# Value products of a chunked attention: from pairs of token tiles to all four at once

## The chip, the cores and the metric

The kernel runs on one core of one Trainium2 chip. The metric is the device time of one execution in microseconds (us). Lower is better. The kernel before was timed three times; its median is 1318.02 us.

A core has engines that run beside each other and meet only at semaphores: TensorE (PE, matrix products; its weight loads are listed as PEld), VectorE (DVE), ScalarE (ACT), GpSimd (POOL) and SyncE (SP, which here issues nearly all transfers). Each takes its instructions in the order in which they are written for it. PE writes its products into PSUM, eight banks of 512 fp32 columns; all else lies in SBUF or in DRAM.

## The reference

One layer of a hybrid encoder over 2048 tokens of width 1024. A normalised input goes through one wide projection, whose columns feed three mixers: chunked softmax attention (6 heads of 64), an mLSTM (6 heads) and gated linear attention (4 heads). Each is gated, the results are put side by side, projected back, added to the input and normalised. The change touches the attention:

```python
# q, k, v: 6 heads of 64; a chunk is 64 tokens; a query sees its own chunk and 8 chunks before it
scores = einsum('bnqhd,bnkhd->bhnqk', qc, kb) * d ** -0.5
scores = where(valid, scores + rel_bias, -1e30)
p = softmax(scores)                       # over up to 9 * 64 keys
o = einsum('bhnqk,bnkhd->bnqhd', p, vb)   # "value products" below
y_a = o * silu(gate)
out = rmsnorm(x + concat(y_a, y_b, y_c) @ w_out)
```

## The kernel before

**Stages.** The 2048 tokens are four quarters (`q` = 0 to 3, `QT` = 512 tokens), each of four token tiles (`tt` = 0 to 3) of 128. In the first stage, which ends at about 913 us of the profiled span, each quarter is projected and the two recurrent mixers run; queries, keys, values and gates are written to DRAM. The second stage is the attention and the output projection. Every fp32 factor is there as two parts, high and low (`FR`, fp32r), and a product is the sum of two or three products of parts.

**Order on PE.** PE's order is the order in which the program emits its instructions (`manual_schedule`, line 134). Generators yield after each piece and `merge(a, b, na, nb)` (line 76) interleaves two of them: a counter starts at 0, goes up by `nb` for a step of `a` and down by `na` for a step of `b`; `a` steps while it is not positive. The order on the other engines is set by a planner that simulates a timeline.

**The attention of one head** has two generators:

- `scores(q, h)` (line 936) loads the head's queries, keys and values, and per token tile makes the products with its keys (line 960): for `q` of 1 to 3 each tile has 640 keys, in two segments of 384 and 256 columns, with a bank of the pool `s` (two banks) each. VectorE adds the bias and takes the maximum (976), ScalarE the exponential and its sum (979), VectorE the reciprocal (980), GpSimd scales the tile `pt` (981). 8 steps for a head.
- `mix(q, h)` (line 1001) takes the four `pt` tiles, transposes their 128x128 blocks on PE into a bank `tp` (1032, three banks), copies it as high part `ph` (1037, ScalarE) and low part `pl` (1038, VectorE), three buffers each, and multiplies them with the values `vv` into the bank `w` (one bank): line 1046 with `ph` and 128 columns of weights, line 1049 with `pl` and 64. When the head is done, its two halves are added into `cc` (1052 on ScalarE, 1053 on VectorE), and after every second head `cc` is gated (1067) and split into the two parts of `Y` (997, 998). A filled `tp` is called a pack; the value products of a pack come two packs after its transposes.

For `q` of 1 to 3 the four token tiles cover eight key blocks of 128: tile `tt` needs the blocks `tt` to `tt + 4`, 20 blocks for a head. Before the change `mix` works on pairs of tiles (0 and 1, then 2 and 3). A block that both tiles of a pair need is one product of 256 columns, any other one of 128. Six packs for a head, of 512, 512 and 256 columns for each pair; 24 value products.

**Groups of heads.** `attention0` does quarter 0 (mixed with the last projections) and the scores of the first head of quarter 1. Then, for `q` = 1, 2, 3, `attention(q)` merges `scores(q, h)` with `mix(q, h - 1)`, and `spread` merges the whole with `out_mm(q - 1)`, the output projection of the quarter before: 64 steps of three products with 512 columns (1099 to 1101), "o" below. `spread` is told how many attention steps there will be (`units * 14 + 8 * (units - 1)`); what it doesn't use up of `out_mm` comes at the end of the quarter, with no attention beside it. `load_y` (1119) then fetches the other mixers' results for the next `out_mm` through two buffers `wraw`, splits them into `Y[3]` to `Y[7]` (997 on ScalarE, 998 on GpSimd), and these take the place of the quarter's before, which the last steps of `out_mm` still read.

Of the kernel before, what the change touches and what calls it, by code (L numbers as in the profile page):

```python
# [11 lines left out]
ALU = mybir.AluOpType  # L12
# [60 lines left out]

def merge(a, b, na, nb):
    acc = 0
    live = True
    while a is not None or b is not None:
        if a is not None and (b is None or acc <= 0):  # L80
            acc += nb
            try:
                next(a)
                yield
            except StopIteration:
                a = None
        elif b is not None:
            acc -= na
            try:
                next(b)  # L90
                yield
            except StopIteration:
                b = None
# [6 lines left out]
def f32(ap):  # L100
    return ap.bitcast(FP32)
# [3 lines left out]
def trunk_kernel(ctx: ExitStack, tc: tile.TileContext, xT, x, w_f, w_t, w_o, w_gates, norm_g, conv_w,  # L105
# [760 lines left out]
    with ExitStack() as pb_:  # L866
# [134 lines left out]
        def mix(q, h, Y, vv, pts, nkb):  # L1001
# [4 lines left out]
                cur["gt"] = big.tile([P, QT], FP32, name="gt")  # L1006
                nc.sync.dma_start(cur["gt"], ga_d[:, h // 2, q * QT:(q + 1) * QT])
            cc, gt = cur["cc"], cur["gt"]
            todo = []
            for pr in range(NC // 2):  # L1010
                pp = pts[2 * pr:2 * pr + 2]
                one_use, two_use = [], []
                for b in range(nkb):
                    use = tuple(tt for tt in range(2) if pp[tt][1] <= b < pp[tt][1] + pp[tt][2])
                    if use:
                        (one_use if len(use) == 1 else two_use).append((b, use))
                packs, width = [], 1024
                for b, use in one_use + two_use:
                    if width + P * len(use) > 512:
                        packs.append([])  # L1020
                        width = 0
                    packs[-1].append((b, use, width))
                    width += P * len(use)
                todo += [(pr, pp, g, pk, g == len(packs) - 1) for g, pk in enumerate(packs)]
            ops = {}

            def turn_(pr, pp, g, pk, last):
                tp = pbank("tp")
                for b, use, w in pk:
                    for x_, tt in enumerate(use):  # L1030
                        pt, b0, _ = pp[tt]
                        nc.tensor.transpose(out=tp[:, w + x_ * P:w + (x_ + 1) * P],  # L1032
                                            in_=pt[:, (b - b0) * P:(b - b0 + 1) * P], identity=ident)
                wd = pk[-1][2] + P * len(pk[-1][1])
                ph = big.tile([P, 512], FR, name="ph", bufs=3)
                pl = big.tile([P, 512], FR, name="pl", bufs=3)
                nc.scalar.copy(ph[:, :wd], tp[:, :wd])  # L1037
                nc.vector.tensor_tensor(pl[:, :wd], tp[:, :wd], f32(ph[:, :wd]), op=ALU.subtract)  # L1038
                return ph, pl

            def pv(pr, pp, g, pk, last, ph, pl):
                if not ops:
                    ops[0] = pbank("w")
                op = ops[0][:, pr * ST:(pr + 1) * ST]
                for e, (b, use, w) in enumerate(pk):
                    nc.tensor.matmul(op[:, use[0] * P:use[0] * P + P * len(use)], vv[:, b, :], ph[:, w:w + P * len(use)],  # L1046
                                     start=(pr == 0 and g == 0 and e == 0), stop=False, skip_group_check=True)
                for e, (b, use, w) in enumerate(pk):
                    nc.tensor.matmul(op[0:64, use[0] * P:use[0] * P + P * len(use)], vv[:, b, 64 * (h % 2):64 * (h % 2) + 64],  # L1049
                                     pl[:, w:w + P * len(use)], start=False, stop=(last and e == len(pk) - 1), skip_group_check=True)  # L1050
                if last and pr == NC // 2 - 1:
                    nc.scalar.copy(cc[mr], ops[0][cr])
                    nc.vector.tensor_tensor(cc[mr], ops[0][mr], cc[mr], op=ALU.add)

            held = []
            for it in todo:
                ph, pl = turn_(*it)
                yield
                held.append(it + (ph, pl))
                if len(held) > 2:  # L1060
                    pv(*held.pop(0))
                    yield
            pv(*held.pop(0))
            yield
            pv(*held.pop(0))
            if h % 2 == 1:
                nc.gpsimd.tensor_tensor(cc, cc, gt, op=ALU.mult)
                Y[h // 2] = split_y(cc, q, h // 2)
# [13 lines left out]
        def attention(q, Y, done):  # L1082
            for h in range(len(done), AH + 1):
                a = scores(q, h, done) if h < AH else None
                b = mix(q, h - 1, Y, *done[h - 1]) if h else None
                yield from merge(a, b, 8, 14)

        def out_mm(q, Y):
            for tt in range(NC):
# [46 lines left out]
        for q in range(1, NQ):  # L1136
            YB = {}
            units = AH + 1 - len(nxt)
            spread(attention(q, YB, nxt), units * 14 + 8 * (units - 1), out_mm(q - 1, YA), YN)
            nxt = []  # L1140
            YA = YB
            for k in (3, 4, 5, 6, 7):
                load_y(q, YA, k)
# [85 lines left out]
```

## Time and profile before

| | |
|---|---|
| median of 3 runs | 1318.02 us (1317.06 to 1320.14) |
| the profiled execution's own time | 1321.42 us |
| its span, from which the profile counts | 1319.7 us |
| PE busy | 1266.8 us (96%) |
| DVE, POOL, ACT busy | 813.0, 630.6, 595.9 us |
| mean granted clock of PE | 0.982 |

Reading it: PE's times are starts and lengths of instructions that overlap each other, as a product's tail runs under the next one's head; what a product costs a full PE is the distance from its start to the start of the next. A wait is shown as `[us <-who released it]`. The number after `x` is how many like instructions were put into one row. PEclk is the granted clock of PE as a share of the full one.

### The profile page before, as it was taken

The numbers are of one execution on the slowest core, as the hardware profiler recorded it, in microseconds if no ns is written. First come the engines' busy times: TensorE is split into PE (matmuls) and PEld (weight loads), VectorE is DVE, ScalarE is ACT, GpSimd is POOL, SyncE is SP. The second block draws the span as 40 slices with busy tenths as digits, with TensorE's granted clock in tenths as the row PEclk, the third lists the DMA queues.
The fourth block names the chain that finished last, engine by engine and source line by source line (L and its number), as shares of the span: only waits on it lengthen the run. The fifth ranks groups of instructions, "written<-read, shape, count | busy, mean of one in ns | idle before, by whom it ended". The sixth has DMA issues, their size and how long they took to land.

```text
span 1319.7 us, 19935 instructions
## 1 busy us (share of the span) xinstructions
PE 1266.8 (96%) x7044; PEld 1038.1 (79%) x7044; DVE 813.0 (62%) x1859; ACT 595.9 (45%) x1124; POOL 630.6 (48%) x847
## 2 busy tenths in 40 slices
PE   4999999999999999999999999999979999999997
PEld 2788777878787788877778787887768888889876
DVE  7626656672775767267666866664467767666711
ACT  5624422463443247244224543332466556556621
POOL 5327652332766225367622656642165454454442
PEclk7999999999999999999999999999889999999999
DMA  7444233634423354442244333328677656565222
GB/s 249 157 120 136 84 104 113 181 121 138 129 80 106 111 183 133 127 134 86 91 127 125 112 102 88 108 69 260 180 221 218 184 176 187 157 206 148 81 95 79
DMA packets 106516, 181.66 MB, mean 138 GB/s; under 512 B 9776, under 2 KB 54704, under 8 KB 106416
## 3 DMA queue, kind: packets, MB, share of 16 engines
q1 hardware_dynamic: 101808, 172.00, 43.6%
q10 hardware_dynamic: 4608, 8.39, 1.7%
q8 instruction: 55, 0.90, 0.3%
q14 instruction: 45, 0.37, 0.1%
HBM read 143.92 MB, written 36.44 MB: 137 GB/s over the span
## 4 chain that ended last, share of the span: by engine, by line
PE 81%; DVE 8%; DMA 3%; ACT 3%; issue 2%; POOL 2%; SPq 1%; POOLq 0%; DVEq 0%; ACTq 0%
PE ip L245 13%; PE ip L247 12%; PE ip L246 12%; PE ip L1101 4%; PE ip L1099 4%; PE ip L1100 4%; PE ip L265 3%; PE s L960 3%; PE ip L267 3%; PE ip L266 3%; PE tp L1032 3%; PE w L1049 2%; PE w L1046 2%; PE ga L748 2%; PE s L600 1%
## 5 line engine op out<-in xcount | busy, mean ns | idle before, releaser
L245 PE MATMUL ip<-x,w 128*128 128x512 f32 x800 | 329.2, 412 | 0.0
L247 PE MATMUL ip<-x,w 128*128 128x512 f32 x800 | 314.4, 393 | 0.0
L246 PE MATMUL ip<-x,w 128*128 128x512 f32 x800 | 313.6, 392 | 0.0
L245 PEld LDWEIGHTS ip<-x,w 128*128 128x128 f32 x800 | 151.3, 189 | 42.0 <-issue 12.9
L247 PEld LDWEIGHTS ip<-x,w 128*128 128x128 f32 x800 | 150.9, 189 | 33.4
L246 PEld LDWEIGHTS ip<-x,w 128*128 128x128 f32 x800 | 151.5, 189 | 29.0 <-issue 2.2
L238 DVE TENSOR_TENSOR w<-wraw,w 128x1024 fp32r<-128x1024 f32 x88 | 122.8, 1395 | 70.0 <-ACT w L237 64.2
L237 ACT CAST w<-wraw 128x1024 fp32r<-128x1024 f32 x132 | 137.9, 1046 | 60.4 <-DMA wraw<-in_w_f 27.6
L238 POOL TENSOR_TENSOR w<-wraw,w 128x1024 fp32r<-128x1024 f32 x44 | 107.8, 2449 | 79.3 <-ACT w L237 79.3
L981 POOL TENSOR_SCALAR pt<-pt,sm 128x640 f32<-128x640 f32 (+2 forms) x96 | 71.2, 743 | 135.8 <-DVE sm L980 110.5
L265 PE MATMUL ip<-w,x 128*128 128x512 f32 x256 | 101.9, 398 | 4.9 <-ACT vg L429 4.7
L267 PE MATMUL ip<-w,x 128*128 128x512 f32 x256 | 99.9, 390 | 0.0
L266 PE MATMUL ip<-w,x 128*128 128x512 f32 x256 | 99.8, 390 | 0.0
L979 ACT ACTIVATE pt<-pt,sm 128x640 f32<-128x640 f32 (+2 forms) x96 | 73.3, 763 | 52.9 <-DVE sm L976 51.8
L691 POOL TENSOR_TENSOR prd<-gk,zg 128x16 f32<-128x16 f32 (+7 forms) x112 | 66.1, 590 | 60.6 <-PE pw L697 55.2
L960 PE MATMUL s<-kk,qq 128*128 128x256 f32 (+2 forms) x360 | 83.9, 320 | 5.7 <-DMA kk<-k_d 2.4
L1038 DVE TENSOR_TENSOR pl<-tp,ph 128x512 fp32r<-128x512 f32 (+2 forms) x126 | 73.9, 597 | 22.8 <-ACT ph L1037 21.5
L1037 ACT CAST ph<-tp 128x512 fp32r<-128x512 f32 (+2 forms) x126 | 63.1, 512 | 41.8 <-PE tp L1032 37.9
L400 ACT ACTIVATE e<-ip 128x512 f32<-128x512 f32 x44 | 26.1, 593 | 122.6 <-PE ip L247 106.3
L960 PEld LDWEIGHTS s<-kk,qq 128*128 128x128 f32 x360 | 63.5, 198 | 16.1 <-issue 5.2
L688 POOL TENSOR_TENSOR gk<-gk,al 128x16 f32<-128x16 f32 (+14 forms) x120 | 71.2, 594 | 8.5 <-ACT al L665 1.3
L470 DVE SCALAR_TENSOR_TENSOR qk<-u,cw,qk 128x512 f32<-128x512 f32 x72 | 69.7, 969 | 8.9 <-ACT qk L468 7.5
(303 smaller groups left out, 2544.8 us busy)
## 6 DMA issues: line engine op xcount, KB each, us to landing
wraw<-in_w_f SPq DMA_DIRECT2D x100, 512.0 KB, 3.6
wraw<-in_w_t SPq DMA_DIRECT2D x32, 512.0 KB, 3.7
qq<-q_d SPq DMA_DIRECT2D x48, 256.0 KB, 5.8
kk<-k_d SPq DMA_DIRECT2D x18, 512.0 KB, 6.8
vv<-v_d SPq DMA_DIRECT2D x18, 512.0 KB, 4.9
xraw<-in_x SPq DMA_DIRECT2D x16, 512.0 KB, 5.9
xraw<-in_xT SPq DMA_DIRECT2D x16, 512.0 KB, 6.8
xr<-in_x SPq DMA_DIRECT2D x16, 512.0 KB, 3.6
```

The lines of the kernel that those rows point to most:

```text
L237: nc.scalar.copy(w[:, :, 0, :], rv)
L238: other().tensor_tensor(w[:, :, 1, :], rv, f32(w[:, :, 0, :]), op=ALU.subtract)
L245: nc.tensor.matmul(ps, w[:, k, 0, :], X[k][:, 0, :], start=(k == 0), stop=False)
L246: nc.tensor.matmul(ps, w[:, k, 0, :], X[k][:, 1, :], start=False, stop=False)
L247: nc.tensor.matmul(ps, w[:, k, 1, :], X[k][:, 0, :], start=False, stop=(k == KT - 1))
L265: nc.tensor.matmul(ps, X[k][:, 0, t], w[:, 0, :], start=(k == 0), stop=False)
L266: nc.tensor.matmul(ps, X[k][:, 0, t], w[:, 1, :], start=False, stop=False)
L267: nc.tensor.matmul(ps, X[k][:, 1, t], w[:, 0, :], start=False, stop=(k == KT - 1))
L688: nc.gpsimd.tensor_tensor(b16(gk)[:, :, 0:c], b16(gk)[:, :, 0:c], b16(al)[:, :, c:c + 1].broadcast_to([P, NB, c]), op=ALU.mult)
L960: nc.tensor.matmul(sp[:, :cn], qq[:, l, tt * P:(tt + 1) * P], kk[:, ko + c0:ko + c0 + cn], start=(l == 0), stop=(l == 1))
L979: nc.scalar.activation(pt[:, :n], pt[:, :n], AF.Exp, bias=init, scale=-1.0, accum_out=sm[:, 2:3])
L1038: nc.vector.tensor_tensor(pl[:, :wd], tp[:, :wd], f32(ph[:, :wd]), op=ALU.subtract)
```

## The change

`mix` no longer works on pairs of tiles. For each of the eight key blocks it lists the tiles that need it (`use`), and a block is one product over all of them: 128, 256, 384, 512, 512, 384, 256, 128 columns for the blocks 0 to 7. The blocks are put into five packs of 512 columns each, in the order [2, 0], [1, 6], [3], [4], [5, 7]; in quarter 0, where there are four blocks of 512, 384, 256 and 128 columns, into [0], [1, 3], [2]. So a head has 16 value products instead of 24 (8 instead of 12 in quarter 0), five casts and subtractions of a pack instead of six (three and three), and as many transposes as before. The first pack needs the tiles 0 to 2, the second all four.

`mix` has 10 steps instead of 12 for `q` of 1 to 3, so `merge` in `attention` is given 10 instead of 14, and a counter that starts at -12: two steps of the scores come ahead of the first step of `mix`. `spread` is told of `units * 10` instead of `units * 14` steps. The bank `w` is taken at the start of `mix`. And the space that is reserved at the bottom of each SBUF partition for descriptors of dynamic DMA, 16,384 bytes by default, is set to 4,096, so what lies above it starts 12,288 bytes lower.

```diff
@@ -73,8 +73,7 @@
 
 
 
-def merge(a, b, na, nb):
-    acc = 0
+def merge(a, b, na, nb, acc=0):
     live = True
     while a is not None or b is not None:
         if a is not None and (b is None or acc <= 0):
@@ -1006,63 +1005,52 @@
                 cur["gt"] = big.tile([P, QT], FP32, name="gt")
                 nc.sync.dma_start(cur["gt"], ga_d[:, h // 2, q * QT:(q + 1) * QT])
             cc, gt = cur["cc"], cur["gt"]
-            todo = []
-            for pr in range(NC // 2):
-                pp = pts[2 * pr:2 * pr + 2]
-                one_use, two_use = [], []
-                for b in range(nkb):
-                    use = tuple(tt for tt in range(2) if pp[tt][1] <= b < pp[tt][1] + pp[tt][2])
-                    if use:
-                        (one_use if len(use) == 1 else two_use).append((b, use))
-                packs, width = [], 1024
-                for b, use in one_use + two_use:
-                    if width + P * len(use) > 512:
-                        packs.append([])
-                        width = 0
-                    packs[-1].append((b, use, width))
-                    width += P * len(use)
-                todo += [(pr, pp, g, pk, g == len(packs) - 1) for g, pk in enumerate(packs)]
-            ops = {}
-
-            def turn_(pr, pp, g, pk, last):
+            use = [[tt for tt in range(NC) if pts[tt][1] <= b < pts[tt][1] + pts[tt][2]] for b in range(nkb)]
+            packs = ([2, 0], [1, 6], [3], [4], [5, 7]) if q else ([0], [1, 3], [2])
+            src, done = {}, []
+            op = pbank("w")
+
+            def turn_(pk):
                 tp = pbank("tp")
-                for b, use, w in pk:
-                    for x_, tt in enumerate(use):
-                        pt, b0, _ = pp[tt]
+                w = 0
+                for b in pk:
+                    for x_, tt in enumerate(use[b]):
+                        pt, b0, _ = pts[tt]
                         nc.tensor.transpose(out=tp[:, w + x_ * P:w + (x_ + 1) * P],
                                             in_=pt[:, (b - b0) * P:(b - b0 + 1) * P], identity=ident)
-                wd = pk[-1][2] + P * len(pk[-1][1])
+                    src[b] = slice(w, w + P * len(use[b]))
+                    w += P * len(use[b])
                 ph = big.tile([P, 512], FR, name="ph", bufs=3)
                 pl = big.tile([P, 512], FR, name="pl", bufs=3)
-                nc.scalar.copy(ph[:, :wd], tp[:, :wd])
-                nc.vector.tensor_tensor(pl[:, :wd], tp[:, :wd], f32(ph[:, :wd]), op=ALU.subtract)
-                return ph, pl
-
-            def pv(pr, pp, g, pk, last, ph, pl):
-                if not ops:
-                    ops[0] = pbank("w")
-                op = ops[0][:, pr * ST:(pr + 1) * ST]
-                for e, (b, use, w) in enumerate(pk):
-                    nc.tensor.matmul(op[:, use[0] * P:use[0] * P + P * len(use)], vv[:, b, :], ph[:, w:w + P * len(use)],
-                                     start=(pr == 0 and g == 0 and e == 0), stop=False, skip_group_check=True)
-                for e, (b, use, w) in enumerate(pk):
-                    nc.tensor.matmul(op[0:64, use[0] * P:use[0] * P + P * len(use)], vv[:, b, 64 * (h % 2):64 * (h % 2) + 64],
-                                     pl[:, w:w + P * len(use)], start=False, stop=(last and e == len(pk) - 1), skip_group_check=True)
-                if last and pr == NC // 2 - 1:
-                    nc.scalar.copy(cc[mr], ops[0][cr])
-                    nc.vector.tensor_tensor(cc[mr], ops[0][mr], cc[mr], op=ALU.add)
+                nc.scalar.copy(ph[:, :w], tp[:, :w])
+                nc.vector.tensor_tensor(pl[:, :w], tp[:, :w], f32(ph[:, :w]), op=ALU.subtract)
+                for b in pk:
+                    src[b] = ph[:, src[b]], pl[:, src[b]]
+
+            def to(b, r=slice(0, P)):
+                return op[r, use[b][0] * P:use[b][0] * P + P * len(use[b])]
+
+            def pv(pk):
+                for b in pk:
+                    nc.tensor.matmul(to(b), vv[:, b, :], src[b][0], start=not done, stop=False, skip_group_check=True)
+                    done.append(b)
+                for b in pk:
+                    nc.tensor.matmul(to(b, slice(0, 64)), vv[:, b, 64 * (h % 2):64 * (h % 2) + 64], src[b][1],
+                                     start=False, stop=(len(done) == nkb and b == pk[-1]), skip_group_check=True)
 
             held = []
-            for it in todo:
-                ph, pl = turn_(*it)
+            for pk in packs:
+                turn_(pk)
                 yield
-                held.append(it + (ph, pl))
+                held.append(pk)
                 if len(held) > 2:
-                    pv(*held.pop(0))
+                    pv(held.pop(0))
                     yield
-            pv(*held.pop(0))
+            pv(held.pop(0))
             yield
-            pv(*held.pop(0))
+            pv(held.pop(0))
+            nc.scalar.copy(cc[mr], op[cr])
+            nc.vector.tensor_tensor(cc[mr], op[mr], cc[mr], op=ALU.add)
             if h % 2 == 1:
                 nc.gpsimd.tensor_tensor(cc, cc, gt, op=ALU.mult)
                 Y[h // 2] = split_y(cc, q, h // 2)
@@ -1083,7 +1071,7 @@
             for h in range(len(done), AH + 1):
                 a = scores(q, h, done) if h < AH else None
                 b = mix(q, h - 1, Y, *done[h - 1]) if h else None
-                yield from merge(a, b, 8, 14)
+                yield from merge(a, b, 8, 10, -12)
 
         def out_mm(q, Y):
             for tt in range(NC):
@@ -1136,7 +1124,7 @@
         for q in range(1, NQ):
             YB = {}
             units = AH + 1 - len(nxt)
-            spread(attention(q, YB, nxt), units * 14 + 8 * (units - 1), out_mm(q - 1, YA), YN)
+            spread(attention(q, YB, nxt), units * 10 + 8 * (units - 1), out_mm(q - 1, YA), YN)
             nxt = []
             YA = YB
             for k in (3, 4, 5, 6, 7):
@@ -1222,7 +1210,7 @@
 
     arrays = _layout(inputs)
     S = arrays["x"].shape[0]
-    nc = _bacc.Bacc("TRN2", target_bir_lowering=False, num_devices=1)
+    nc = _bacc.Bacc("TRN2", target_bir_lowering=False, num_devices=1, dynamic_dma_scratch_size=4096)
     _build(nc, arrays, S)
     r = _run(nc, [{f"in_{n}": v for n, v in arrays.items()}], core_ids=[0])
     return r.results[0]["out_0"].reshape(1, S, D)
```

## The prediction

> **What bounds the kernel now.** I read the page's head and chain, then the busy times by stage, PE's waits, and PE's instructions in order of time.
>
> ```profile
> span 1319.7 us, 19935 instructions
> PE 81%; DVE 8%; DMA 3%; ACT 3%; issue 2%; POOL 2%; SPq 1%; POOLq 0%; DVEq 0%; ACTq 0%
> ```
>
> ```profile
> 913.00:995.00 82.00, 70.13 (x367) 59.92 (x367) 46.18 (x150) 44.11 (x101) 31.66 (x38) 0.85 0.77 229
> ...
> 1078.00:1169.00 91.00, 88.49 (x552) 77.77 (x551) 61.47 (x183) 54.33 (x119) 45.21 (x47) 1.00 0.62 176
> ...
> 1262.00:1312.00 50.00, 47.21 (x195) 37.02 (x193) 8.99 (x21) 10.45 (x23) 17.41 (x17) 0.97 0.25 85
> ```
>
> After each stretch and its length come the busy times of PE, PEld, DVE, ACT and POOL, PEclk, DMA share and GB/s. PE is the chain. Where the attention runs beside the output projection (the middle row, quarter 2) PE is busy for 88.5 of 91 us, DVE for 61.5, ACT for 54.3, POOL for 45.2. So only two things can move the time: PE's own work, and its waits.
>
> ```profile
> PE w L1049 <- DVE pl L1038: 5.5, 6, 2.7
> PE w L1046 <- DVE cc L1053: 2.8, 1, 2.8
> PE s L960 <- DMA kk<-k_d: 2.4, 1, 2.4
> ...
> PE ip L1099 <- ACT y L997: 2.0, 1, 2.0
> PE ip L1101 <- POOL y L998: 1.7, 2, 1.1
> PE s L960 <- DVE sm L976: 1.3, 1, 1.3
> PE tp L1032 <- POOL pt L981: 0.8, 1, 0.8
> ```
>
> These are PE's waits from 913 us on (total, times, longest). They are few and sit at borders: at the front, where quarter 0 passes into quarter 1, and wherever one quarter ends. Between the borders a head runs without any.
>
> **The products.** PE's order within quarter 2:
>
> ```profile
> 1090.39 0.60 PE L1032 MATMUL tp<-ident,pt 128*128 128x128 f32 x4
> 1090.75 0.49 PE L960 MATMUL s<-kk,qq 128*128 128x256 f32 x2
> 1091.07 0.40 PE L1099 MATMUL ip<-x,hl 128*128 128x512 f32 x1
> ...
> 1091.77 0.38 PE L1032 MATMUL tp<-ident,pt 128*128 128x128 f32 x2
> 1091.91 0.59 PE L1046 MATMUL w<-ph,vv 128*128 128x128 f32 x3
> 1092.33 0.40 PE L1049 MATMUL w<-pl,vv 128*64 128x128 f32 x3
> 1092.57 0.39 PE L1099 MATMUL ip<-x 128*128 128x512 f32 x1
> ...
> 1094.75 0.39 PE L1046 MATMUL w<-ph,vv 128*128 128x256 f32 x2
> 1094.98 0.40 PE L1049 MATMUL w<-pl,vv 128*64 128x256 f32 x2
> 1095.22 0.40 PE L960 MATMUL s<-kk,qq 128*128 128x256 f32 x2
> ```
>
> From start to start: three projection products of 512 columns take 0.70 us (1091.07 to 1091.77), 0.233 each. Two value products of 256 columns take 0.23 with `ph` and 0.24 with `pl`: the same per column, so joining 256 and 256 to 512 saves nothing. Three products of 128, 128 and 256 columns (one pack) take 0.24 with `pl`, again the same, but 0.42 with `ph`. Of that, 0.08 is the start behind a transpose (the score pair behind the four transposes takes 0.32, the pair at 1095.22, like every pair that follows no transpose, 0.24). That leaves 0.34 against 0.23, so a 128-column product with the 128-column weights costs 0.055 more than its columns. Before, a head has four of these (blocks 0, 5, 2, 7 of the pairs), after, two (blocks 0 and 7): 18 heads x 2 x 0.055 = 2.0 us. Quarter 0 goes from two to one: 6 x 0.055 = 0.3. **Products: -2.3 us**, bounds -3 and -1, since no value product of 384 columns or more stands in the trace; the nearest row is the 512-column one.
>
> [...]
>
> **Transposes**: 20 for a head as before. Four take 0.36 and two 0.14, each group with 0.08 behind it: 4 x 0.44 + 2 x 0.22 = 2.2 before, 5 x 0.44 = 2.2 after. Nothing. **Casts and subtractions**: 126 become 108, with the same columns; DVE and ACT each save about 3 us, hidden under PE. If that cover were gone, they would be worth the 3 us. **The bank `w`**, taken earlier in the program, has one user at a time as before: nothing.
>
> **Steps moved.** I counted out both orders from `merge`. S is the score pair of 256 columns, Sa that of 384, T transposes, V value products, o three projection products. From the last scores of a head to the first transposes that need its tile 3:
>
> ```
> before: S3 o Sa T1 o T2 S0 o T3 V1 o Sa T4
> after:  S3 o V4 V5 o Sa S0 o T1 Sa o T2
> ```
>
> With Sa 0.35, S 0.24, o 0.70, V 0.47 to 0.52, T 0.36 and 0.08 behind each T, that is 5.6 us before and 5.4 after. What has to fit in is the softmax of tile 3:
>
> ```profile
> 1101.34 0.40 PE L960 MATMUL s<-kk,qq 128*128 128x256 f32 x2
> ```
>
> ```profile
> 1103.68 0.80 POOL L981 TENSOR_SCALAR pt<-pt,sm 128x640 f32<-128x640 f32 x1 [2.60 <-DVE sm L980]
> ```
>
> 1101.34 to 1104.48, 3.1 us: no wait in a middle head, with 2.3 us to spare. At the borders it is tighter.
>
> *First head of quarter 1.* T2 now comes 3.9 us behind S3 (before 6). The chain there:
>
> ```profile
> 994.04 0.40 PE L960 MATMUL s<-kk,qq 128*128 128x256 f32 x2
> ```
>
> ```profile
> 996.90 1.30 POOL L1067 TENSOR_TENSOR cc<-cc,gt 128x512 f32<-128x512 f32 x1
> 998.17 1.25 POOL L981 TENSOR_SCALAR pt<-pt,sm 128x640 f32<-128x640 f32 x1
> ```
>
> ```profile
> 1002.32 0.45 PE L1049 MATMUL w<-pl,vv 128*64 128x256 f32 x2 [0.65 <-DVE pl L1038]
> ...
> 1139.66 0.45 PE L1049 MATMUL w<-pl,vv 128*64 128x256 f32 x2 [0.28 <-DVE pl L1038]
> ...
> 1230.12 0.45 PE L1049 MATMUL w<-pl,vv 128*64 128x256 f32 x2 [0.28 <-DVE pl L1038]
> ```
>
> The chain takes 5.4 us, as POOL does other work first. New wait 1.5; the wait of 0.7 for `pl` at 1002.32 goes, as V comes later. **+0.8**, bounds 0 and +3.
>
> *Last head of quarters 2 and 3.* With no scores beside it, T2 comes S3 0.24, o 0.70, V4 and V5 0.99, o 0.70, T1 0.36 = 3.0 us behind S3. The chain:
>
> ```profile
> 1154.74 0.40 PE L960 MATMUL s<-kk,qq 128*128 128x256 f32 x2
> ```
>
> ```profile
> 1157.34 0.80 POOL L981 TENSOR_SCALAR pt<-pt,sm 128x640 f32<-128x640 f32 x1 [2.80 <-DVE sm L980]
> ```
>
> 3.4 us: a wait of 0.4 in each. **+0.8**, bounds 0 and +2. Behind a waiting T stands all of PE: the next o, then the scores.
>
> *End of a quarter.* The count that `spread` was told was too high (7 x 14 + 48 = 146 against 48 + 6 x 12 = 120 steps for quarters 2 and 3): 11 of the 64 o's came alone at the end. After, 118 against 108: five come alone; in quarter 1 none. Each o moves forward with its load of `xr` on SP and its two stores on ACT's queue; SP passes them ahead of a few loads of the next heads, which have microseconds to spare.
>
> At the end of quarter 1 the waits for `sm` and `pt` (1.3 and 0.8) come from DVE and POOL work of the last o's in a rush of four score tiles. The gating and splitting of the last head now fall into that rush: about 1.6 left, **-0.5**, bounds -2 and +1.5. At the end of quarter 2 `Y[7]` gets about 2 us more: its wait of 1.1 nearly goes, **-1.0**, bounds -1.1 and +1. At the end of quarter 3:
>
> ```profile
> 1262.05 2.55 POOL L998 TENSOR_TENSOR y<-wraw,y 128x512 fp32r<-128x512 f32 x2
> ```
>
> ```profile
> 1266.44 0.62 ACT L997 CAST y<-wraw 128x512 fp32r<-128x512 f32 x1 [2.23 <-DMA wraw<-y_d]
> ```
>
> ```profile
> 1267.11 0.50 PE L1099 MATMUL ip<-w,y 128*128 128x512 f32 x1 [1.96 <-ACT y L997]
> 1267.45 0.40 PE L1100 MATMUL ip<-w,y 128*128 128x512 f32 x1
> 1268.47 0.68 PE L1101 MATMUL ip<-w,y 128*128 128x512 f32 x1 [0.62 <-POOL y L998]
> ```
>
> ```profile
> 1268.60:1272.00 3.40, 3.40 (x8) 2.43 (x9) 0.00 (x0) 0.00 (x0) 1.13 (x1) 0.50 0.63 188
> ```
>
> `Y[6]` is late: POOL's first split ends at 1263.33, the refill of that buffer lands 3.1 us later. Behind the wait of 2.6 come 3.4 us at clock 0.50, which cost 1.7. After, old `Y[3]` is free 6.8 us ahead of the next quarter's first o instead of 4.9. From that moment: split of `Y[3]` on POOL done at 2.6 (behind one operation of 1.3), `Y[4]` 3.9, gating of the last head 6.2, `Y[5]` 7.5, refill for `Y[7]` at 10.6, cast 11.2, split 12.5. PE wants `Y[7]` at 6.8 + 4 x 0.70 = 9.6: waits of 1.6 and 0.8, on `Y[7]` instead of `Y[6]`, and half of a slow stretch, as 1.3 us of wait brought none and 2.0 one. 2.4 + 0.85 against 2.6 + 1.7: **-1.0**, bounds -4.3 and +1.5.
>
> [...]
>
> The waits for `pl` at 1139.66 and 1230.12, 0.3 each, go, as T and V stand further apart: **-0.6**, bounds -0.6 and 0.
>
> **The reserve for DMA descriptors**: the trace has no transfer on POOL's queue; nothing. It moves the second stage's tiles in SBUF, so some may be free earlier (a rival below).
>
> **Sum**: -2.3 + 0.8 + 0.8 - 0.5 - 1.0 - 1.0 - 0.6 = **-3.8 us**. The profiled execution took 1321.4 (span 1319.7, 1.7 around it), so 1317.6 for its like; the median of the runs is 1318.0, 3.4 below the profiled one, and I put the same difference against it: **1314.2 us**.
>
> **Rivals.** *The borders give nothing*: the waits only change their owners, and the products alone count, or less: 1318.0 - 2.3 + 1.3 = 1317. For it: the refill through two buffers stays. Against: fewer o's stand alone.
>
> *Tile 3 decides at every head* (slower). The second pack needs all four tiles where before the first three needed two. The softmax chain has 5.4 us; the sum turns at 5.4 + 3.8/15 = 5.7 for the 15 middle heads. At 6.0 us it costs 15 x 0.6 = 9: 1314.2 + 9 = 1323. For it: 5.4 us at 994. Against: 3.1 at 1101, and DVE and ACT are relieved.
>
> ```profile
> 985.30:992.20 6.90, 5.08 (x23) 4.98 (x24) 4.92 (x13) 3.29 (x8) 4.56 (x5) 0.51 1.07 338
> ```
>
> *The front clears*: the row from 913 to 995 has 11.9 us without PE work and a clock of 0.85. The longest waits there are for `cc` and `pl`, 2.8 and 2.7. Other addresses and shorter DVE queues could remove one, with a slow stretch like this row's behind it: 2.8 + 3.4 = 6.2 more, 1308. Against: the transfers and splits of the output weights that crowd it are unchanged.
>
> *It does not do what it says*: the 128-column excess belongs to something else in these packs, and the waits balance: 1318.
>
> **The numbers.** Forecast 0.50 (1309 to 1318 by its bounds), borders give nothing 0.20, tile 3 0.14, front 0.12, nothing 0.04. The range of 1304.5 to 1321 takes in all but the far ends of the front and tile 3. About 0.2% (2.6 us) is what a measurement can tell from no change: faster means below 1315.4, slower above 1320.6. Faster: 0.34 of the forecast, 0.05 of the borders, the front's 0.12 = 0.51; slower: 0.14 + 0.03 = 0.17; the same: 0.32.
>
> **What would show it.** Products: 0.47 for a full pack in the middle, 0.53 where it holds a 128. T2 waiting on POOL at the first head of quarter 1 and the last of 2 and 3, and at no middle head; a middle-head wait makes the third rival right. No `Y` wait at the end of quarters 1 and 2, one on the fifth o of the last. A changed busy share from 913 to 995 would mean that the front moved, for which I have no term.

## The result, and the profile after

The changed kernel takes **1325.92 us** (median; 1325.00 to 1327.09) beside 1318.06 for the kernel before: ratio 1.0058, 95% interval 1.0041 to 1.0075. By the ratio it is slower by 7.7 us; I had forecast 1314.2 and a range from 1304.5 to 1321. Its profiled execution took 1327.09 us.

The head of its page, and its stretches of time from the first scores of quarter 1 to those of quarters 2 and 3, to the first output step of the last projection, and to the end. After the stretch and its length come the busy times of PE, PEld, DVE, ACT and POOL, PEclk, DMA share and GB/s.

```profile
span 1325.4 us, 19502 instructions
```

```profile
982.53:1089.50 106.97, 97.09 (x540) 81.44 (x541) 68.44 (x187) 62.26 (x128) 54.53 (x52) 0.96 0.69 195
1089.50:1179.03 89.53, 86.92 (x506) 74.55 (x505) 58.94 (x177) 53.60 (x111) 44.32 (x46) 1.00 0.58 178
1179.03:1269.60 90.57, 88.44 (x505) 75.77 (x504) 59.70 (x176) 54.66 (x113) 45.96 (x48) 0.98 0.44 135
1269.60:1325.40 55.80, 45.05 (x193) 35.67 (x191) 11.27 (x24) 11.79 (x26) 18.67 (x18) 0.97 0.23 80
```

The same four stretches of the kernel before:

```profile
979.34:1080.82 101.48, 96.99 (x597) 85.89 (x597) 70.93 (x193) 63.17 (x135) 54.26 (x53) 0.95 0.70 210
1080.82:1171.99 91.17, 88.66 (x554) 77.96 (x553) 61.16 (x182) 53.96 (x118) 45.76 (x48) 1.00 0.61 175
1171.99:1262.50 90.51, 88.91 (x553) 77.81 (x552) 60.95 (x182) 54.27 (x119) 45.59 (x48) 1.00 0.44 128
1262.50:1319.70 57.20, 46.71 (x193) 36.65 (x191) 10.44 (x24) 11.77 (x26) 18.68 (x18) 0.94 0.25 83
```

PE's work fell: the sum of its four busy times is 317.50 against 321.27. But quarter 1 is 5.5 us longer with the same work, so PE stood still there for 9.9 us instead of 4.5. From the first scores of quarter 1 on, the two executions differ by 342.87 - 340.36 = 2.5 us. The other 3.2 us lie ahead of it and begin with the first projection product:

```profile
31.75 0.50 PE L245 MATMUL ip<-x,w 128*128 128x512 f32 x1
```

```profile
34.28 0.50 PE L244 MATMUL ip<-x,w 128*128 128x512 f32 x1
```

No changed instruction has run by then, and the runs below put the start down to the execution. In those runs the changed kernel without its reserve and two near variants (output steps put back; two buffers in a place of their own) are 4.6 to 5.2 us slower than before.

PE's waits in the changed kernel from the first scores of quarter 1 (total, times, longest):

```profile
PE w L1035 <- ACT ph L1025: 5.5, 3, 2.4
PE s L959 <- DVE sm L975: 5.0, 4, 2.1
PE w L1038 <- DVE pl L1026: 2.3, 3, 1.7
PE tp L1019 <- POOL pt L980: 2.0, 3, 0.8
PE ip L1089 <- POOL hl L997: 1.8, 1, 1.8
PE ip L1087 <- ACT hl L996: 1.2, 1, 1.2
```

Before, the waits for `sm` came to 1.3. The waits of 2 us and more stand at three places. The first is the beginning of quarter 1, on ACT and then on PE:

```profile
984.31 1.05 ACT L930 CAST w<-wraw 128x1024 fp32r<-128x1024 f32 x1 [3.62 <-DMA wraw<-in_w_o]
985.38 0.58 ACT L1052 COPY cc<-w 64x512 f32<-64x512 f32 x1
...
988.26 0.80 PE L1035 MATMUL w<-ph,vv 128*128 128x512 f32 x1 [2.44 <-ACT ph L1025]
...
990.75 0.69 PE L1038 MATMUL w<-pl,vv 128*64 128x512 f32 x1 [1.69 <-DVE pl L1026]
```

ACT stands 3.6 us at the cast of a late output weight, which waits for its transfer. Behind it in ACT's order stand the copy `cc<-w`, which frees the bank `w`, and the next head's casts `ph`. Before, the copy came ahead of that cast:

```profile
979.94 0.58 ACT L1052 COPY cc<-w 64x512 f32<-64x512 f32 x1
981.14 1.04 ACT L931 CAST w<-wraw 128x1024 fp32r<-128x1024 f32 x1 [0.62 <-DMA wraw<-in_w_o]
```

The second place is the end of quarter 1, where the same happens with the refills of `load_y`:

```profile
1086.18 0.62 ACT L996 CAST y<-wraw 128x512 fp32r<-128x512 f32 x1 [5.42 <-DMA wraw<-y_d]
1086.70 0.58 ACT L1025 CAST ph<-tp 128x512 fp32r<-128x512 f32 x1
...
1090.88 0.62 ACT L996 CAST hl<-wraw 128x512 fp32r<-128x512 f32 x1 [2.60 <-DMA wraw<-y_d]
```

```profile
1087.33 0.49 PE L1035 MATMUL w<-ph,vv 128*128 128x512 f32 x1 [2.15 <-ACT ph L1025]
...
1093.63 0.50 PE L959 MATMUL s<-kk,qq 128*128 128x256 f32 x2 [1.59 <-DVE sm L975]
...
1097.48 0.50 PE L959 MATMUL s<-kk,qq 128*128 128x256 f32 x2 [1.01 <-DVE sm L975]
```

ACT waits 5.4 us for a refill, with the last head's `ph` behind it, and PE waits for that `ph`. Then the next quarter's scores crowd on VectorE, which itself stands 1.5 us for ACT's copy `cc<-w` at 1091.53, behind the cast of the last refill. Before, ACT waited for a refill here too, but with the last head's `ph` done since 1074.5:

```profile
1080.04 0.62 ACT L997 CAST y<-wraw 128x512 fp32r<-128x512 f32 x1 [2.44 <-DMA wraw<-y_d]
```

The rows of the changed kernel show ACT taking its instructions in order: the transposes of the last head's fourth pack stand on PE at 1081.82, 0.60 long, but the pack's `ph` starts at 1086.70, only behind the cast that waited 5.42.

The third place is the start of quarter 3, a wait of 2.1 for `sm` with a slow stretch behind it:

```profile
1181.65 0.62 ACT L996 CAST y<-wraw 128x512 fp32r<-128x512 f32 x1 [1.12 <-DMA wraw<-y_d]
1182.18 0.62 ACT L1094 ACTIVATE jk<-xr 128x512 f32<-128x512 f32 x1
1182.92 0.94 DVE L1098 TENSOR_TENSOR sm<-sm 128x1 f32<-128x1 f32 x1 [1.89 <-ACT jk L1094]
1184.58 1.14 PE L959 MATMUL s<-kk,qq 128*128 128x384 f32 x4 [2.12 <-DVE sm L975]
```

```profile
1186.00:1189.50 3.50, 3.50 (x12) 3.05 (x11) 2.94 (x9) 2.08 (x6) 3.34 (x4) 0.51 0.10 15
```

VectorE stands in order at the sums of the output stage (the maximum over the scores of 1181.01 starts behind them, at 1183.97), whose square ACT delivers late, because ACT first stands 1.1 us at a cast that waits for a refill. So the refills are at work here as well. Clock 0.51 for 3.5 us of work costs 1.7.

### The profile page after: what moved, and what is told of

Same layout as the page of the kernel before. It is cut to its first block, busy times and chain, and to the rows that moved or that the text cites. A ratio compares the mean times of both kernels' runs of the same rounds, so it can differ in the third digit from the quotient of the medians.

```text
span 1325.4 us, 19502 instructions
## 1 busy us (share of the span) xinstructions
PE 1261.0 (95%) x6876; PEld 1024.3 (77%) x6876; DVE 805.7 (61%) x1841; ACT 594.9 (45%) x1106; POOL 627.1 (47%) x847
## 4 chain that ended last, share of the span: by engine, by line
PE 71%; DVE 10%; DMA 6%; ACT 4%; POOL 4%; issue 4%; POOLq 0%; SPq 0%; ACTq 0%; DVEq 0%
PE ip L244 11%; PE ip L246 10%; PE ip L245 10%; PE ip L1089 3%; PE ip L1087 3%; PE ip L1088 3%; PE s L959 3%; PE ip L264 3%; PE ip L266 3%; PE ip L265 3%; PE tp L1019 3%; PE ga L747 2%; DVE qk L469 2%; PE w L1038 2%; DMA xraw<-in_x 1%
## 5 line engine op out<-in xcount | busy, mean ns | idle before, releaser
L1026 DVE TENSOR_TENSOR pl<-tp,ph 128x512 fp32r<-128x512 f32 (+1 forms) x108 | 71.8, 672 | 40.9 <-ACT ph L1025 40.5
L1025 ACT CAST ph<-tp 128x512 fp32r<-128x512 f32 (+1 forms) x108 | 60.3, 572 | 46.5 <-PE tp L1019 46.1
```

## The experiments

Two theories stood at the start. *Reserve*: the moved addresses cost the start and the front. *Borders*: the new counts put the refills and the output steps at a worse place. Later runs brought in the packs of quarter 0 and the plan of the other engines. Times are given as the ratio to the kernel before on the same chip, with the 95% interval; 0.001 is 1.3 us.

**The reserve alone**, and the change without it:

```diff
-    nc = _bacc.Bacc("TRN2", target_bir_lowering=False, num_devices=1)
+    nc = _bacc.Bacc("TRN2", target_bir_lowering=False, num_devices=1, dynamic_dma_scratch_size=4096)
```

> The kernel before with one line changed: the space reserved for descriptors of dynamic DMA is 4,096 bytes instead of 16,384, and all tiles lie 12,288 bytes lower. In the trace of the change 2.5 us are lost ahead of the first projection product and 2.6 us more at a wait for kk at 934 us, where no changed instruction has run. Theory 'reserve': the moved addresses cause both; then this kernel takes about 1318 + 5 = 1323 us and has the first projection product near 34.3 us. Theory 'borders': the time is lost where quarters end, and the reserve costs nothing; then 1318 us (1316.5 to 1319.5), and the late start is one of this execution only.

> The kernel of the change with the reserve at its default of 16,384 bytes. Theory 'reserve': about 1326 - 5 = 1321 us, with the first projection product near 31.8 us and a kk wait of about 2.4 us at the front. Theory 'borders': 1326 us (1324.5 to 1327.5), with the same waits at the ends of the quarters as the kernel of the change.

Measured: 1.0001 (0.9990 to 1.0012), and 1.0035 (1.0021 to 1.0049). The reserve costs nothing. In the kernel before with the reserve the first projection product came at 31.88, not near 34.3:

```profile
31.88 0.50 PE L245 MATMUL ip<-x,w 128*128 128x512 f32 x1
```

So the 2.5 us at the start belong to that execution. In the changed kernel without the reserve it came at 31.20, and the loss stayed.

**The counts alone**, on the old packs; run again later beside its partner:

```diff
-                yield from merge(a, b, 8, 14)
+                yield from merge(a, b, 8, 12, -12)
-            spread(attention(q, YB, nxt), units * 14 + 8 * (units - 1), out_mm(q - 1, YA), YN)
+            spread(attention(q, YB, nxt), units * 12 + 8 * (units - 1), out_mm(q - 1, YA), YN)
```

> The kernel before (pairs of tiles, six packs, 24 products) with the changed kernel's way of counting: merge with 8 and 12 and a counter that starts at -12, and spread told of units * 12 + 8 * (units - 1), so that no o is left at the end of quarter 1 and about six at the ends of quarters 2 and 3. Theory 'borders': 1318 + 6 to 8 = 1324 to 1326 us, with new waits behind the ends of quarters 1 and 2. Theory 'reserve': 1318 us, since the counts cost nothing.

> Again pairs of tiles under the new counts with the two shared buffers, now on the same chip as its partner. If the new packs pay with two buffers too, it is 4 to 5 us slower than its partner; if they pay nothing, within 2 us of it.

Measured: 1.0036 (1.0025 to 1.0047), and 1.0033 (1.0018 to 1.0048). With not one value product changed, the counts cost 4.4 to 4.8 us: "borders" holds, with less than the 6 to 8 that I gave it.

**The left-over output steps put back**, in the changed kernel:

```diff
-            spread(attention(q, YB, nxt), units * 10 + 8 * (units - 1), out_mm(q - 1, YA), YN)
+            spread(attention(q, YB, nxt), units * 12 + 8 * (units - 1), out_mm(q - 1, YA), YN)
```

> The kernel of the change with one number changed: the count told to spread is units * 12 + 8 * (units - 1) instead of units * 10 + 8 * (units - 1). Eleven to twelve output steps of the 64 then stand alone at the end of quarters 2 and 3 and seven in quarter 1, about as before the change, instead of five and none. Theory 'borders': the six o's that moved out of the end of quarter 1 took away the cover under which load_y's refills and the next quarter's first scores ran; with them back, the waits of 2.2, 1.6 and 1.0 us at 1087 to 1098 and the wait of 2.1 with the slow stretch of 1.7 at 1185 go, and the kernel takes about 1326 - 8 = 1318 us; 1316 if the products give their 2.3 us as well. Theory 'reserve': no change, 1325 to 1326 us, as the loss lies ahead of 935 us.

Measured: 1.0038 (1.0024 to 1.0052), no gain beside the change without its reserve (1.0035). Its wait for `ph` at the end of quarter 1 is gone, and PE waits for the same refills further on, as output steps of the next quarter:

```profile
1089.80 0.50 PE L1089 MATMUL ip<-w,y 128*128 128x512 f32 x1 [0.86 <-POOL y L997]
...
1093.27 0.50 PE L1089 MATMUL ip<-w,hl 128*128 128x512 f32 x1 [1.92 <-POOL hl L997]
```

My theory in that form fell: it isn't the number of steps left over, but the refills through two buffers, that is late either way.

**Five buffers for the refills**, and two in the same new place as a control:

```diff
-            raw = wraws.tile([P, D], FP32, name="wraw")[:, 0:QT]
+            raw = latep.tile([P, QT], FP32, name="yraw", bufs=5)
```

> The kernel of the change, with load_y's two shared buffers wraw replaced by five of its own, so that all five transfers of a quarter can land ahead of time and no cast or split of Y waits for a refill. Nothing else changes, and PE's order is the same. Theory 'refill in ACT's order': at the end of quarter 1 and at the end of quarter 3 ACT stands at a cast that waits for a refill, and the casts ph of the last head behind it; then the waits of 2.2 us at 1085, of 1.2 and 1.8 at 1273 to 1277 and the slow stretches behind them (1.4) go, 5 to 6.5 us in all, and the kernel comes out 0 to 2 us slower than before. Theory 'rush': the first scores of the next quarter crowd on VectorE whatever the refills do; the waits for sm grow by what the others lose, and the kernel stays 3 to 5 us slower than before.

> The kernel of the change with load_y's buffers in a place of their own, but two as before: a control for the run with five, whose plan for the other engines differs from the first stage on. Theory 'refill': it is the third to fifth buffer that pays; this stays 4 to 7 us slower than before. Rival 'another plan': the gain of 11 us came from the new plan and not from the refills; then it is 4 to 7 us faster than before, like the run with five.

Measured: five **0.9945** (0.9931 to 0.9960), two 1.0039 (1.0026 to 1.0051). Five buffers of 2 KB in a partition turn 5 us slower into 7 us faster than before, outside both of my ranges, and the control says that it is their number that pays, not the new place. With five, the casts at the end of quarter 1 run without a wait for a transfer:

```profile
1075.16 0.62 ACT L996 CAST y<-yraw 128x512 fp32r<-128x512 f32 x1
...
1077.03 1.08 ACT L1025 CAST ph<-tp 128x512 fp32r<-128x512 f32 x2
```

PE's waits for `Y` and the slow stretch at the start of quarter 3 are gone in that trace too. The gain of 12 us is about twice what I had expected. The two traces show where it lies, as PE's order is the same in both. Counted from the first scores of quarter 1, the run with five reaches the same product 4.3 us sooner than the control by 1015 us, 8.3 behind the end of quarter 1, 10.8 behind the start of quarter 3, and 14.2 in the last projection. So about 10 us are gained at the three ends of quarters, where the refills stand; beside the trace of the changed kernel it is also 10. The first 4.3 (1.4 beside the changed kernel) lie at the front, ahead of any refill of `load_y`. They go with the other plan or the execution, which the control doesn't separate from the number of buffers.

**Five buffers in the kernel before**, and in the old packs under the new counts: the same edit of `load_y`, without and with the edit of the counts above.

> The kernel before (pairs, old counts) with load_y's two shared buffers replaced by five of its own, and the reserve at 4,096 bytes, which by itself changed nothing. Theory 'refill': the kernel before pays for the refills too, with 2.6 us of waits and 1.7 of a slow stretch at the start of the last projection and 1.1 at the end of quarter 2; it comes out 5 to 6 us faster than before. Rival 'only in the new order': before, the o's left alone at the end of a quarter covered the refills, and it gains less than 2 us.

> Pairs of tiles in all quarters under the new kind of counts (merge with 8 and 12 and a counter from -12, spread told of units * 12 + 8 * (units - 1)), with five buffers of load_y's own and the reserve at 4,096 bytes. Against the run with both cures it differs in the packs of quarters 1 to 3 alone. By the rows of the value products (17.1 us for a quarter with pairs, 14.5 with the new packs) the new packs are worth 7 us, so this kernel should be 3 to 5 us faster than before, 7 slower than the run with both cures. By the sum in my prediction (2.9 us for the products and the short waits for pl) it should be within 3 us of the run with both cures.

Measured: 0.9985 (0.9972 to 0.9997), and **0.9930** (0.9916 to 0.9944). Under the old order the buffers bring 2.0 us (0.4 to 3.7), so the rival holds about, though not for its reason: PE's waits for `Y` nearly go there too (0.5 us in place of 3.7), but POOL is now busy with the splits of `Y` and the last gating right up to the first softmax tiles of the next quarter, and the transposes wait for POOL (the same at the start of quarter 3, 3.6 us in all in place of 0.8):

```profile
1088.58 1.30 POOL L998 TENSOR_TENSOR x<-cc,x 128x512 fp32r<-128x512 f32 x1
...
1090.37 3.28 POOL L981 TENSOR_SCALAR pt<-pt,sm 128x640 f32<-128x640 f32 x4
```

```profile
1091.22 0.33 PE L1032 MATMUL tp<-ident,pt 128*128 128x128 f32 x1 [1.15 <-POOL pt L981]
```

Under the new counts they bring 14 us (1.0036 to 0.9930), more than I had expected anywhere. So the counts cost 4.7 with two buffers and gain 7 with five. Of the two expectations for the second run, the one from the rows of the value products missed (it is 9.2 us faster than before, not 3 to 5), and the one from my prediction's sum holds: the run with both cures, below, is 9.0 faster.

**Quarter 0 on pairs**, the rest of the change as it is; run again later beside the counts alone:

```diff
-                b = mix(0, h - 2, Y, *done[h - 2]) if h >= 2 else None
+                b = mix0(0, h - 2, Y, *done[h - 2]) if h >= 2 else None
```

`mix0` is `mix` of the kernel before; the last two heads of quarter 0 take it too.

> The kernel of the change, but the six heads of quarter 0 keep the pairs of token tiles (packs of 384, 384 and 512 columns, 12 products, the first pack needing tile 1 only). Theory 'quarter 0': the waits for ph and pl from 983 to 998 us, 6.2 us in the two traces of the new packs beside 4.3 before, come from packs of quarter 0 that stand at another place among the casts of the late weights; then 2 to 4 us of the loss go and the kernel is 1 to 3 us slower than before. Theory 'late weights': ACT stands at those casts whatever the packs are; then it stays 4 to 5 us slower than before.

> Again the kernel of the change with pairs in quarter 0, the partner of the run before. By the rows of the value products less the waits of transposes, the packs of quarters 1 to 3 are worth 2 to 4 us here; by the pair with five buffers, nothing; by the first measurement of this pair, 5 us.

Measured: 0.9998 (0.9984 to 1.0012), and 1.0001 (0.9987 to 1.0015). Beside the change without the reserve (1.0035), the new packs of quarter 0 cost 4.9 us, so "quarter 0" holds in kind, and for more than I gave it. Side by side with the counts alone (1.0033) the packs of quarters 1 to 3 are worth 4.2 us, with about 2.8 of uncertainty.

**The old order with the new packs**, then also with pairs in quarter 0:

```diff
-                yield from merge(a, b, 8, 10, -12)
+                yield from merge(a, b, 8, 14)
-            spread(attention(q, YB, nxt), units * 10 + 8 * (units - 1), out_mm(q - 1, YA), YN)
+            spread(attention(q, YB, nxt), units * 14 + 8 * (units - 1), out_mm(q - 1, YA), YN)
+            for _ in range(2 if q else 0):
+                yield
             held = []
```

> The new packs and products under the old counts: merge with 8 and 14 and a counter from 0, spread told of units * 14 + 8 * (units - 1), and two empty steps ahead of each head's first transposes in quarters 1 to 3, so that mix has 12 steps again and every scores step and every o stands at the step it had before. Eleven o's are left alone at an end of quarters 2 and 3. Theory 'order': the counts cost the 4.7 us that they cost the old packs, and the new packs save 3 to 4 us of PE's work; then the kernel is 1 to 4 us faster than before. Theory 'packs': the new packs lose at the front what they save later; then it is within 1.5 us of before. My theory on record, that the products alone count, gives 2.3 faster.

> As the run with the old counts, and the heads of quarter 0 on pairs as before, so that the program up to the first scores of quarter 1 is the one before: only products of quarters 1 to 3 differ. Theory 'order': 3 to 4 us faster than before, from 18 heads that each save 0.19 us of PE's work, two thirds of it beyond the 0.11 of my sum. Theory 'quarter 0': faster than the run with the old counts alone by 2 us or more. If neither shows, the value products save less than the trace of the change suggests.

Measured: 1.0062 (1.0041 to 1.0082), and 1.0027 (1.0015 to 1.0039). Quarter 0 shows again, as expected of it (4.6 us between them). All else that I had written down missed: I had both down as no more than 1.5 us slower than before, and they are 8.2 and 3.6 slower. What the trace shows of it is the place of the transposes; from the first scores of quarter 1, the run with pairs in quarter 0 has

```profile
PE tp L1019 <- POOL pt L980: 7.2, 9, 1.6
```

where the changed kernel has 2.0: the new packs need tile 3 early, and under the old order nine packs wait for POOL's `pt`, up to 1.6 us each. The new packs need the new counts.

**Both cures**, the edit of `load_y` with five buffers and the edit for quarter 0, in the changed kernel:

> The kernel of the change with both cures: five buffers of load_y's own, and the heads of quarter 0 on pairs. If the two losses are separate, the gains add: 7 us faster than before for the buffers, as measured, and 3 to 5 more for quarter 0, so 10 to 12 us faster. If quarter 0's waits went already with the other plan that came with the five buffers (4.9 us of waits from 986 to 1003 there instead of 6.6), it is 6 to 8 us faster, as with the buffers alone.

Measured: **0.9932** (0.9919 to 0.9945), 9.0 us faster than before, between the two expectations. The gains don't add. With five buffers, the plan has the copy ahead of the late weight's cast with either kind of pack; here, with pairs:

```profile
981.04 0.58 ACT L1110 COPY cc<-w 64x512 f32<-64x512 f32 x1 [1.80 <-PE w L1107]
...
982.36 1.04 ACT L930 CAST w<-wraw 128x1024 fp32r<-128x1024 f32 x1
```

Against the pairs in all quarters (0.9930), which differs in the packs of quarters 1 to 3 alone, nothing is left of the new packs that the times could tell (0.3 us slower, with about 2.4 of uncertainty). Quarters 2 and 3, first with the new packs, then with pairs:

```profile
1083.71:1171.85 88.14, 87.00 (x507) 74.55 (x506) 59.13 (x177) 54.69 (x113) 44.22 (x47) 1.00 0.58 174
1171.85:1260.11 88.26, 87.20 (x506) 74.34 (x505) 58.44 (x176) 53.94 (x112) 45.66 (x48) 1.00 0.44 132
```

```profile
1079.88:1168.96 89.08, 87.85 (x554) 77.68 (x553) 60.22 (x183) 54.69 (x119) 43.84 (x46) 1.00 0.60 179
1168.96:1257.39 88.43, 87.80 (x554) 77.78 (x553) 59.65 (x182) 54.16 (x118) 45.69 (x48) 1.00 0.46 131
```

The new packs save 0.85 and 0.60 of PE's busy time, and 1.1 us of the two quarters' length.

**Three scores steps ahead**, on top of both cures:

```diff
-                yield from merge(a, b, 8, 10, -12)
+                yield from merge(a, b, 8, 10, -22)
```

> The run with both cures, and merge's counter starts at -22 instead of -12, so that three steps of the scores instead of two come ahead of a head's first transposes. Theory 'tile 3': the value products save what their rows say, and transposes that wait for tile 3 give it back: 1.1 us at the first head of quarter 1, 0.4 at the third, 0.9 at the first of quarter 3 and 1.2 at the last of quarter 1. The first three go, and the kernel is 2 us faster than the run with both cures, 10.5 to 11.5 us faster than before. Rival: the waits pass on to the scores or to the value products, and it stays 9 us faster than before.

Measured: 0.9947 (0.9927 to 0.9968), 7.0 us faster than before (4.2 to 9.6). That leaves out the 10.5 to 11.5 of "tile 3", and the rival's 9 lies within. These are two of PE's waits from the first scores of quarter 1 on, with both cures and then with three steps ahead:

```profile
PE tp L1019 <- POOL pt L980: 2.1, 3, 0.8
PE s L959 <- DVE sm L975: 1.6, 3, 1.0
```

```profile
PE s L959 <- DVE sm L975: 5.0, 7, 1.5
...
PE tp L1019 <- POOL pt L980: 0.4, 1, 0.4
```

The transposes gain 1.7 us and the scores lose 3.4.

## Why the prediction was wrong

**Products: right in size, lucky in the count.** I let the two 128-column products that remain keep their excess of 0.055 each. The rows bear that out, but not where I had put it:

```profile
1080.62 0.39 PE L1035 MATMUL w<-ph,vv 128*128 128x384 f32 x2
1080.85 0.40 PE L1038 MATMUL w<-pl,vv 128*64 128x384 f32 x2
1081.08 0.44 PE L1087 MATMUL ip<-w,hl 128*128 128x512 f32 x1
1081.36 0.40 PE L1088 MATMUL ip<-w,hl 128*128 128x512 f32 x1
```

A pack of 384 and 128 columns takes 0.23 with `ph` and 0.23 with `pl`, like any other. But from the first product of the o behind it to the second it takes 0.28 instead of 0.23. So it is on average behind 20 such packs between 1020 and 1260 us; behind packs that don't end with a 128-column product it is 0.23. As these rows and those of before read, the excess arises where 128 columns of weights are loaded *behind* a 128-column product, and it shows at the product that has these weights. Before, four `ph` products of a head stand so. After, no `ph` product does, but the last `pl` product of two packs does, with an o or a score pair behind it. Four and two are the numbers that I had used, so the forecast of 2.0 us for quarters 1 to 3 stands, and that the second number was right for another product than I meant is luck. The measurements agree with it: 1.45 of busy time in two quarters, where the forecast makes 1.3; in the times 4.2 ± 2.8 with two buffers and -0.3 ± 2.4 with five, which by themselves leave the worth of the packs open.

**Tile 3.** No middle head waits, as I said. At the first head of quarter 1 PE waits 0.81 for tile 2, which the first pack needs, and 0.39 for tile 3, where I had 1.5 for tile 3 alone:

```profile
1002.74 0.44 PE L1019 MATMUL tp<-ident,pt 128*128 128x128 f32 x2 [0.81 <-POOL pt L980]
```

The wait of 0.65 for `pl` behind it is gone, as I had it, so this term is +0.6 in place of +0.8. The last heads of quarters 2 and 3 don't wait at all (I had +0.8). The last head of quarter 1 does, where I had no such wait; it is counted below, with that end:

```profile
1079.32 0.77 PE L1019 MATMUL tp<-ident,pt 128*128 128x128 f32 x5 [0.75 <-POOL pt L980]
```

The two waits of 0.3 for `pl` at 1139.66 and 1230.12 are gone, as forecast.

**"End of a quarter": the step that failed.** I counted only how much earlier the old `Y` comes free, and gave -0.5 and -1.0 for the ends of quarters 1 and 2. At the end of quarter 1 the waits went from 2.1 (`sm` and `pt`) to 2.15 + 1.59 + 1.01 + 0.75 (`pt`), which is +3.4; at the end of quarter 2 from 1.1 to 2.1 with 1.7 of slow stretch, +2.7. Both are outside my bounds. What I left out is that a refill's cast has a place in ACT's order, and that with no output step left alone the last head's casts `ph` stand behind it. I had named the two buffers as an argument for a rival, and followed the refills one by one only at the end of quarter 3; at the other two ends I never asked which cast is queued in front of whom. The sign that I had named, no wait for `Y` at the ends of quarters 1 and 2, came true all the same: a late refill shows there as waits for `ph` and `sm`. The term for the end of quarter 3 was right in place and near in size: waits of 1.2 and 1.8 for `Y[7]` (the last two rows of the table), no slow stretch, 3.0 in place of 2.6 + 1.7, so -1.3 against -1.0. The three ends come to +4.8 by these traces; the counts alone were measured at +4.4 to +4.8.

**Quarter 0: no term at all** beyond -0.3 for its products. Its packs cost 4.6 to 4.9 us, measured twice. What the traces show of it is ACT's order at the late weight: in the five traces of new packs in quarter 0 with two buffers the copy stands behind that cast, in the twelve others ahead of it. The place of the cost can be read by asking when two traces with the same order in quarters 1 to 3 reach the same product. The change without its reserve is 1.0 us behind the run with pairs in quarter 0 at 913 us, 5.7 behind at 1020, and 5.2 in the last projection; for the two runs under the old order it is also 1.0, then 4.4 and 5.5; with five buffers, where the copy comes first with either kind of pack, 0.5, 0.3 and 0.3. These are single executions, but both pairs with two buffers put the cost between 913 and 1020 us, and it is gone where the copy comes first. That ACT's order is the cause isn't shown by a run that changes it alone, and why the plan turned isn't known.

**Reserve: nothing**, as predicted. **"The front clears"** did not come, and what moves there moves from one execution to the next.

**The range.** The bounds that I gave to the terms, added straight, reach from 1307 to 1326; the range of 1304.5 to 1321 stops short of them at its upper end.

Put together, in us against before, by the ratios: counts +4.7 (1.0036), packs of quarters 1 to 3 -5.0 (to 0.9998), packs of quarter 0 +4.9 (to 1.0035), reserve 0: **+4.6** on the chips of the experiments. These are steps from one kernel to the next, so their sum is that of the change without its reserve by construction, and no check. The first comparison gave 7.7, with an interval of ± 2.2; I can't place the other 3.

## What to carry to other kernels

A closer interleave takes away cover as well as slack: before you shorten a tail of lone work, list which transfers land under it and which in-order engine casts them. Where a cast that waits for a transfer can be planned ahead of work on the critical path, give the transfer its own buffers first; here that was worth 12 us, three times what I had forecast for the change, some 10 of it where the refills stand. And measure the order and the arithmetic of a change apart: here the order cost 4.7 us or gained 7, by the buffers beside it.

## What the runs showed of the hardware

The wait of 2.12 us that ended at 1184.58 was followed by 3.5 us at a mean clock of 0.51 (1186.0 to 1189.5), while behind those of 2.15 at 1087.33 and 1.81 at 1276.52, in the last projection, the clock stayed at 1.00 for 10 us. In the kernel before, the wait of 1.96 at 1267.11, with one of 0.62 behind it, was followed by 3.4 us at 0.50. In these traces the length of the wait alone doesn't decide. A 128-column product took 0.06 or 0.11 us by the weights that are loaded behind it: three products of 128, 128 and 256 columns take 0.34 with `ph` and 0.24 with `pl`, and the first product of an o behind a `pl` product of 128 columns takes 0.28 instead of 0.23. In the trace of before, the row of a load of 128 columns is 0.19 us long (line 1099 at 1093.94), and the load behind it starts 0.11 later (line 1100 at 1094.05), which agrees with the 0.11 of the product.
